# Three edits to the queues of a hybrid layer: 32 constant products, and weight splits and loads that stand behind others

## The chip, the core and the metric

The kernel runs on one core of a Trainium2 chip. A core has five engines with a queue of instructions each: PE (TensorE, matrix products), DVE (VectorE), ACT (ScalarE), POOL (GpSimd) and SP (SyncE), which here only issues DMA transfers. The metric is the device time of one execution in microseconds (us).

## What is computed

One layer of a diffusion backbone on 1024 latent tokens of 1024 channels, with 256 context tokens. Cut to what matters here:

```python
shift, scale, gate = jnp.split(jax.nn.silu(c) @ w_mod[i] + b_mod[i], 3, axis=-1)
mod_c = jax.nn.silu(c_ctx) @ w_mod[i] + b_mod[i]
h = _layer_norm(x) * (1.0 + scale[:, None]) + shift[:, None]
hc = _layer_norm(ctx) * (1.0 + mod_c[D_MODEL:2 * D_MODEL]) + mod_c[:D_MODEL]
u_ctx = hc @ w_in[i][:, :D_SSM] + b_in[i][:D_SSM]
_, ctx_final = _s5_bidir(u_ctx, discs, ssm_c_re[i], ssm_c_im[i], ssm_d[i], None, False)
ua, za, ub, vb, zb, ga, gb = _split_proj(h @ w_in[i] + b_in[i])
y_a, _ = _s5_bidir(ua, discs, ssm_c_re[i], ssm_c_im[i], ssm_d[i], ctx_final, True)
ya = _ssm_glu_gate(y_a, za, glu_w[i], glu_b[i])
yb = _sgu_branch(ub, vb, zb, sgu_ln_g[i], sgu_ln_b[i], sgu_w[i], sgu_b[i], lat_chunks)
out = _merge_out(ya, yb, ga, gb, w_branch_a[i], w_branch_b[i], w_out[i], b_out[i])
x = _layer_norm(DEEPNORM_ALPHA * x + gate[:, None] * out) * ln_g[i] + ln_b[i]
```

`_s5_bidir` is a linear recurrence over the positions, once in each direction (S5). `ua` is its input, `za` its gate.

## The kernel before

Every float32 product is made of three: a value is split into a rounded high half (`hh`, `h_blk`, `uw` 0) and the rest as a low half (`hl`, `l_blk`, `uw` 1), and PE adds high times high, high times low and low times high (L82 to L84). ACT writes the high half of a split and DVE the low half behind it (L77, L78). `modulate` does the same for the rows of the activations: ACT scales and shifts (`hf`), ACT rounds (`hh`), DVE takes the rest (`hl`).

The program begins with loads of x, of the modulation weights `wm` and of the weights for `ua` (`uw`, in four quarters of 256 channels each). While these arrive, PE multiplies constants (`warm`, L455). Then `ua` is computed in steps k = 0 to 7 over 128 channels each, for the first half of the tokens (`ua_step(k, 0)`), and for the second half after it. Ahead of a step's rows stand its modulation: products `pm` on PE, a copy `mrow` on DVE, products `pmc` on PE, an addition `mods` on DVE. A step k uses quarter k/2 of `uw`; `load_uw` loads and splits quarters 1 to 3 in the course of steps 0, 1 and 3. Beside it DVE normalises x tiles 4 to 7 (BATCH_NORM_STATS2 at L185, the normalisation at L197) and prepares the recurrence (`disc`). A later stage does the context.

The recurrence runs on DVE while PE does the products of the other branch. Its readout has four blocks b (`y_mm(b)`): PE multiplies `um` (rows of u, read back from DRAM by `y_rows`) by `mt`, and the states `z` by the tables `ca` (from DRAM by `y_tables`), into `py`. ACT applies GELU from `py` to `gk`, and PE transposes `gk` into `pg` (`y_trans`). `y_states` copies the states to `z` on ACT and DVE. Behind the readout come the products `pp` for `za`, with blocks of weights `r_blk` split to `h_blk` and `l_blk` in the order in which `job` lists them; `weights(key, ahead)` splits all jobs up to `ahead` behind `key`.

The order in which an engine's queue holds its instructions is not that of the text: a scheduler of the tool chain sets it when the program is built. A block under `tc.issue_after(i)` holds instructions that must stand behind instruction i. Loads use rotating buffers (three of RAW, four of TMP, six of WSP), and a load on SP's queue waits until its buffer is free; what stands behind it on SP waits too.

Of the kernel before, what the change touches and what calls it, by code (L numbers as in the profile page):

```python
# [8 lines left out]
F32 = mybir.dt.float32  # L9
F32R = mybir.dt.float32r  # L10
I32 = mybir.dt.int32
AF = mybir.ActivationFunctionType
OP = mybir.AluOpType
# [14 lines left out]
UB, ZB, ZA, GA, GB = 0, 4, 8, 12, 20  # L28
# [8 lines left out]
def mixer_kernel(ctx: ExitStack, tc: tile.TileContext, a, out):  # L37
    nc = tc.nc
    V, S, Pl, PE = nc.vector, nc.scalar, nc.gpsimd, nc.tensor
# [21 lines left out]
    def BANK(name, shape=(128, 512)):  # L61
        return psum.tile(list(shape), F32, name=name, tag="b", bufs=8)

    def dma(o, i):
        return nc.sync.dma_start(o, i)
# [9 lines left out]
    def split(hi, lo, src, eng=None):  # L75

        first = S.activation(hi, src, AF.Copy)  # L77
        return first, (eng or V).tensor_tensor(lo, src, hi.bitcast(F32), op=OP.subtract)  # L78
# [13 lines left out]
    def emit_load():  # L92
        key, ap, shape, eng = jobs[emitted[0]]
        emitted[0] += 1
        raw = RAW("r_" + key, shape)
        dma(raw, ap)
        hi, lo = WSP("h_" + key, shape), WSP("l_" + key, shape)
        split(hi, lo, raw, eng)
        loaded[key] = (hi, lo)

    def weights(key, ahead=2):
        i = [j[0] for j in jobs].index(key)
        while emitted[0] < min(i + 1 + ahead, len(jobs)):
            emit_load()
        return loaded[key]
# [98 lines left out]
    hth = [None] * 8  # L204
    htl = [None] * 8

    def modulate(dh, dl, src, k, n):

        w = src.shape[-1]
        f = TMP("hf")[:, :w]  # L210
        S.activation(f, src, AF.Identity, bias=mods[:, k, 0, n:n + 1], scale=mods[:, k, 1, n:n + 1])
        S.activation(dh, f, AF.Copy)  # L212
        V.tensor_tensor(dl, f, dh.bitcast(F32), op=OP.subtract)

    pms = {}

# [29 lines left out]
    def trans_mod(k, hf):  # L246
        sl = slice(hf * 512, hf * 512 + 512)
        modulate(hth[k][:, sl], htl[k][:, sl], pts[k, hf], k, 0)
# [6 lines left out]
    uw = BIG("uw", (128, BIG0 + 8192), F32R)[:, BIG0:].rearrange("p (s q j n) -> p s q j n", s=2, q=4, j=2)  # L255

    def load_uw(q):
        raw = RAW(f"uw{q}", (128, 2, 512))
        dma(raw, a["w_ua"][q])
        split(uw[:, 0, q], uw[:, 1, q], raw, V)  # L260

    def split_uw0(j):
        return split(uw[:, 0, 0, j], uw[:, 1, 0, j], uwr[:, j], V)
# [87 lines left out]
    q, w, z, sn, cs, odd, eve, sg = (r_[i] for i in range(3, 11))  # L351
# [99 lines left out]


    warm = BANK("warm")
    for i in range(44):
        PE.matmul(warm[:, 0:128], ones, ident, start=True, stop=True)  # L455
    with tc.issue_after(folded.ins):
        for t in range(3):
# [13 lines left out]
    for k in range(8):  # L471
        if k >= 6:
            trans_h(k - 6, 1)
        ua_step(k, 0)
        if k + 2 < 8:
            load_wm(k + 2)

            for t in {2: (4,), 3: (5,), 4: (6, 7)}.get(k, ()):
                load_x(t)
            if k in (0, 1, 3):  # L480
                load_uw((k + 3) // 2)
            trans_pe(k + 2, 0)
            mod(k + 2)
            trans_mod(k + 2, 0)
        for t in {3: (4,), 4: (5,), 5: (6, 7)}.get(k, ()):
            norm_here(t)
        issue(8 if k < 5 else 4)

    xc = []
    for j in range(2):  # L490
        t = RAW(f"xc{j}")
# [5 lines left out]
    def trans_c(k):  # L497
        p = BANK(f"pc{k}")
        for j in range(2):
            PE.transpose(p[:, j * 128:(j + 1) * 128], xc[j][:, k * 128:(k + 1) * 128], ident)  # L500
        modulate(cth[k // 4][:, k % 4, :], ctl[k // 4][:, k % 4, :], p[:, :256], k, 1)
# [26 lines left out]
    for b in range(4):  # L528
        p = BANK(f"pcu{b}")
# [277 lines left out]
            then(t, p, sl)  # L807


    ca_last, cas, mts, ums, zs, gks, gt = {}, {}, {}, {}, {}, {}, []  # L810

    def y_tables(b):
        for d in range(2):
            ca = WSP(f"ca{b}{d}", (128, 8, 8, 16), F32)
            ca_last[b] = dma(ca.rearrange("p g i h -> p (g i h)"), cad[b, d])
            cas[b, d] = ca
        mts[b] = RAW(f"mt{b}", (128, 8, 128))
        if b == 3:

            with tc.issue_after(ca_last[2].ins):  # L820
                dma(mts[b], mtd[b])
        else:
            dma(mts[b], mtd[b])
        if b < 2:
            y_rows(b)

    def y_rows(b):
        src = ud[b].rearrange("t (h g) c -> (t h) g c", g=8)[:, :, 32:160]
        if b < 2:
            t = ROW(f"um{b}", (128, 8, 128))  # L830
            dma(t, src)
            ums[b] = [t[:, g, :] for g in range(8)]
        else:
            ts_ = [TMP(f"um{b}{h}", (128, 4, 128)) for h in range(2)]
            for h, t in enumerate(ts_):
                dma(t, src[:, 4 * h:4 * h + 4])
            ums[b] = [ts_[g // 4][:, g % 4, :] for g in range(8)]

    def y_states(b):
        for d in range(2):  # L840
            zt = G(f"z{b}{d}", (128, 8, 128))
            o = 31 if d == 0 else 33
            for cp in range(2):
                for par in range(2):
                    dst = zt[64 * cp:64 * cp + 64, par:8:2, :]
                    src = vst[64 * par:64 * par + 64, d, o:o + 128, cp, 4 * b:4 * b + 4].rearrange("p c q -> p q c")
                    if par == 0 and cp == 0:
                        S.activation(dst, src, AF.Copy)
                    else:
                        V.tensor_copy(dst, src)  # L850
            zs[b, d] = zt

    def y_mm(b):
        gks[b] = G(f"gk{b}", (128, T, 128))
        for h in range(2):
            p = BANK(f"py{b}{h}", (128, 4, 128))
            for i in range(4):
                g = 4 * h + i
                PE.matmul(p[:, i, :], ums[b][g], mts[b][:, g, :], start=True, stop=False)
                for d in range(2):  # L860
                    PE.matmul(p[:, i, :], zs[b, d][:, g, :], cas[b, d][:, g].rearrange("p i h -> p (i h)"),
                              start=False, stop=d == 1)
            S.activation(gks[b][:, :, 64 * h:64 * h + 64].rearrange("p t (g h) -> p g t h", h=16),
                         p.rearrange("p g (t h) -> p g t h", h=16), AF.Gelu_apprx_tanh)

    def y_trans(b):
        g_ = G(f"gT{b}")
        for h in range(2):
            p = BANK(f"pg{b}{h}")
            for i in range(4):  # L870
                PE.transpose(p[:, 128 * i:128 * i + 128], gks[b][:, 4 * h + i, :], ident)
            dst = g_.rearrange("p (c t) -> p t c", t=T)[:, 4 * h:4 * h + 4, :]
            src = p.rearrange("p (t c) -> p t c", t=4)
            if h == 0:
                S.activation(dst, src, AF.Copy)
            else:
                V.tensor_copy(dst, src)
        gt.append(g_)
# [18 lines left out]
        if i == 6:  # L897
            y_tables(0)

    y_rows(2)  # L900
    y_rows(3)
    for b in range(4):
        y_mm(b)
        if b < 3:
            y_states(b + 1)
        if b < 2:
            y_tables(b + 2)
        if b > 0:
            y_trans(b - 1)
    y_trans(3)  # L910

# [197 lines left out]
    for i in range(0, 8, 2):  # L1111
# [15 lines left out]
        if i == 0:  # L1127

            for h in range(2):
                p = BANK(f"pga{h}")  # L1130
# [141 lines left out]
```

## Time and profile before

| | |
|---|---|
| median of 3 runs | 718.58 us (718.18 to 720.86) |
| profiled execution | 721.4 us, span 719.6 us, mean granted clock 0.991 |
| PE busy | 700.4 us, 97% of the span |
| DVE, ACT, POOL busy | 529.4 us (74%), 248.8 us (35%), 92.6 us (13%) |
| DMA | 101.98 MB, 142 GB/s on average |

The rows that follow come from the profiled execution; its time lies 1.8 us outside the span. Times are in us from the start of the span.

### The profile page before, as it was taken

The page shows a single profiled execution, that of the slowest core. Times are in us where ns is not written, and L with a number is a line of the kernel's source. Part 1 is how long each engine was busy: PE and PEld are TensorE (multiplying, and loading weights), DVE is VectorE, ACT ScalarE, POOL GpSimd, SP SyncE. Part 2 cuts the span into 40 slices and gives each one's busy share as a digit, 9 for nine tenths or more (in the row PEclk, how much of TensorE's full clock was granted, in tenths as well). Part 3 has the DMA queues.
Part 4 walks back from the last instruction along what each step waited for, and adds up shares of the span by engine and source line. Part 5 has one row for each costly group of instructions (what it writes and reads, how often), then busy time and mean ns, then how long its engine had stood idle before and what let it go on. Part 6 is the DMA issues. An engine that isn't in the chain of part 4 may idle for free.

```text
span 719.6 us, 10385 instructions
## 1 busy us (share of the span) xinstructions
PE 700.4 (97%) x3964; PEld 587.3 (82%) x3964; DVE 529.4 (74%) x1148; ACT 248.8 (35%) x360; POOL 92.6 (13%) x145
## 2 busy tenths in 40 slices
PE   9899999999999999999999999999999999999993
PEld 8677898888888888888888898888888878888883
DVE  5489945479889485898988489736678569953993
ACT  4328828741014423111112265414353522310000
POOL 1001142007633000000000000001111000000220
PEclk9999999999999999999999999999999999999997
DMA  7960463625721220121213752234567950251421
GB/s 301 383 231 1 108 170 125 184 89 172 232 64 54 94 88 30 59 89 58 89 60 118 243 205 97 84 125 154 175 203 291 411 205 31 93 172 58 174 90 59
DMA packets 41394, 101.98 MB, mean 142 GB/s; under 512 B 8960, under 2 KB 17792, under 8 KB 41344
## 3 DMA queue, kind: packets, MB, share of 16 engines
q1 hardware_dynamic: 35072, 84.04, 33.9%
q0 software_dynamic: 6272, 17.28, 7.2%
q8 instruction: 31, 0.51, 0.3%
q14 instruction: 19, 0.16, 0.1%
HBM read 79.31 MB, written 24.08 MB: 144 GB/s over the span
## 4 chain that ended last, share of the span: by engine, by line
PE 87%; DVE 5%; DMA 3%; ACT 3%; issue 1%; SPq 0%; POOL 0%; DVEq 0%; ACTq 0%
PE pp L82 10%; PE pp L83 10%; PE pp L84 10%; PE po L1168 4%; PE po L1167 4%; PE po L1166 4%; PE pb L84 4%; PE pb L83 4%; PE pb L82 4%; PE pg L82 4%; PE pg L83 4%; PE pg L84 4%; PE pv L580 3%; DMA uw<-in_w_ua 3%; PE pvb L732 2%; PE pvb L733 2%
## 5 line engine op out<-in xcount | busy, mean ns | idle before, releaser
L82 PE MATMUL pp<-hh,h_blk 128*128 128x512 f32 x320 | 125.3, 392 | 0.0
L83 PE MATMUL pp<-hh,l_blk 128*128 128x512 f32 x320 | 124.6, 389 | 0.0
L84 PE MATMUL pp<-hl,h_blk 128*128 128x512 f32 x320 | 124.5, 389 | 0.0
L82 PEld LDWEIGHTS pp<-hh,h_blk 128*128 128x128 f32 x320 | 60.1, 188 | 13.1 <-ACT vst L582 0.4
L84 PEld LDWEIGHTS pp<-hl,h_blk 128*128 128x128 f32 x320 | 60.1, 188 | 12.6
L83 PEld LDWEIGHTS pp<-hh,l_blk 128*128 128x128 f32 x320 | 60.1, 188 | 12.1
L642 DVE TENSOR_TENSOR scm<-acat,vst 128x128 f32<-128x128 f32 x158 | 46.0, 291 | 9.8 <-ACT vst L582 5.0
L77 ACT ACTIVATE h_blk<-r_blk 128x1024 fp32r<-128x1024 f32 x20 | 21.2, 1061 | 53.7 <-PE pp L83 21.7
L646 DVE TENSOR_TENSOR vst<-vst,scs 128x64 f32<-128x64 f32 x158 | 35.3, 224 | 4.9
L645 DVE TENSOR_TENSOR scs<-scm 128x64 f32<-128x64 f32 x158 | 35.4, 224 | 4.6
L78 DVE TENSOR_TENSOR l_blk<-r_blk,h_blk 128x1024 fp32r<-128x1024 f32 x20 | 24.5, 1225 | 17.7 <-ACT h_blk L77 17.6
L1166 PE MATMUL po<-wobig,mh 128*128 128x512 f32 (+1 forms) x90 | 32.9, 365 | 0.0
L1167 PE MATMUL po<-wobig,mh 128*128 128x512 f32 (+1 forms) x90 | 32.9, 365 | 0.0
L1168 PE MATMUL po<-wobig,ml 128*128 128x512 f32 (+1 forms) x90 | 32.9, 365 | 0.0
L82 PE MATMUL pu<-hh,uw 128*128 128x512 f32 x64 | 27.5, 429 | 3.3 <-ACT hh L212 3.3
L1178 DVE TENSOR_TENSOR r<-po,xr 128x512 f32<-128x512 f32 (+1 forms) x18 | 11.0, 618 | 22.1 <-PE po L1168 22.1
L796 ACT ACTIVATE act<-pp,cols 128x512 f32<-128x512 f32 x16 | 10.9, 678 | 46.5 <-issue 19.0
L69 POOL DMA_DIRECT2D md<-mb x8 | 4.3, 543 | 168.1 <-DVE scs L645 110.7
L84 PE MATMUL pu<-hl,uw 128*128 128x512 f32 x64 | 25.9, 408 | 0.0
L83 PE MATMUL pu<-hh,uw 128*128 128x512 f32 x64 | 25.9, 405 | 0.0
L82 PE MATMUL pb<-yas,h_w_a 128*128 128x512 f32 x64 | 25.3, 395 | 0.0
L733 PE MATMUL pvb<-l_vb,hh 128*128 128x512 f32 x64 | 25.0, 391 | 0.0
(413 smaller groups left out, 1733.1 us busy)
## 6 DMA issues: line engine op xcount, KB each, us to landing
r_blk<-in_w_blk SPq DMA_DIRECT2D x20, 512.0 KB, 3.5
wm<-in_wm SPq DMA_DIRECT2D x16, 512.0 KB, 8.9
x<-in_x SPq DMA_DIRECT2D x8, 512.0 KB, 6.0
cad<-kca POOLq DMA_DIRECT2D x8, 512.0 KB, 3.5
md<-mb POOLq DMA_DIRECT2D x8, 512.0 KB, 3.2
ca<-cad SPq DMA_DIRECT2D x8, 512.0 KB, 5.0
ga<-in_w_blk SPq DMA_DIRECT2D x8, 512.0 KB, 3.5
wgt<-in_w_gate SPq DMA_DIRECT2D x8, 512.0 KB, 3.7
```

Of the source, the lines that this page charges most:

```text
L78: return first, (eng or V).tensor_tensor(lo, src, hi.bitcast(F32), op=OP.subtract)
L82: PE.matmul(o, wh, rh, start=first, stop=False, skip_group_check=more)
L83: PE.matmul(o, wl, rh, start=False, stop=False, skip_group_check=more)
L84: PE.matmul(o, wh, rl, start=False, stop=last, skip_group_check=more)
L580: PE.matmul(p[64 * par:64 * par + 64, c, 0:160], abt[:, 2 * q + par, 64 * c:64 * c + 64], u160[b][:, 2 * q + par, :], start=True, stop=True)
L642: V.tensor_tensor(scm, acat.rearrange("p d (o c) q -> p d o (c q)", o=2), both(n - 1, prev).unsqueeze(2).to_broadcast([128, 2, 2, 32]), op ...
L645: V.tensor_tensor(scs4, m4[:, :, 0, :], m4[:, :, 1, :], op=OP.add)
L646: V.tensor_tensor(both(n, 160 if n == 31 else cur), both(n, cur), scs2, op=OP.add)
L733: PE.matmul(pvb[kk], hth[k][:, ks], wl[:, j, :], start=False, stop=False)
L1166: PE.matmul(p, mh, wh, start=k == 0, stop=False)
L1167: PE.matmul(p, mh, wl, start=False, stop=False)
L1168: PE.matmul(p, ml, wh, start=False, stop=k == 7)
```

## The change

It makes four edits. The series of constant products has 32 instead of 44. The splits of `uw` quarters 1 to 3 must stand behind the last `hh` and the last `hl` that `modulate` has issued so far; their loads don't. The loads of u's rows for blocks 2 and 3 must stand behind the loads of the tables of block 1. In the last pass of the readout's loop `weights` is called for the first block of za's weights (which that point of the program has already split), and the next two blocks are split behind the last `gk` of block 3. (In the changed file all lines behind L207 stand 2 to 9 further down.)

```diff
+    rounded = []
+
     def modulate(dh, dl, src, k, n):
...
-        S.activation(dh, f, AF.Copy)
-        V.tensor_tensor(dl, f, dh.bitcast(F32), op=OP.subtract)
+        rounded.append(S.activation(dh, f, AF.Copy))
+        rounded.append(V.tensor_tensor(dl, f, dh.bitcast(F32), op=OP.subtract))
...
     def load_uw(q):
         raw = RAW(f"uw{q}", (128, 2, 512))
         dma(raw, a["w_ua"][q])
-        split(uw[:, 0, q], uw[:, 1, q], raw, V)
+
+        with tc.issue_after(rounded[-2].ins), tc.issue_after(rounded[-1].ins):
+            split(uw[:, 0, q], uw[:, 1, q], raw, V)
...
     warm = BANK("warm")
-    for i in range(44):
+    for i in range(32):
         PE.matmul(warm[:, 0:128], ones, ident, start=True, stop=True)
...
-            S.activation(gks[b][:, :, 64 * h:64 * h + 64].rearrange("p t (g h) -> p g t h", h=16),
+            gk_last[b] = S.activation(gks[b][:, :, 64 * h:64 * h + 64].rearrange("p t (g h) -> p g t h", h=16),
                          p.rearrange("p g (t h) -> p g t h", h=16), AF.Gelu_apprx_tanh)
...
-    y_rows(2)
-    y_rows(3)
+    with tc.issue_after(ca_last[1].ins):
+        y_rows(2)
+        y_rows(3)
     for b in range(4):
+        if b == 3:
+            weights(f"blk{ZA}", 0)
         y_mm(b)
...
     y_trans(3)
+    with tc.issue_after(gk_last[3].ins):
+        weights(f"blk{ZA}", 2)
```

What stands on ACT's queue in the first steps, before: `uw` with 1024 columns is a split of a quarter, `hf` and `hh` are rows of a step.

```order
8 L211 ACTIVATE hf<-pt_207,mods 128x512
9 L212 ACTIVATE hh_205<-hf 128x512
10 L77 ACTIVATE uw<-uw_272 128x1024
11 L211 ACTIVATE hf<-pt_226,mods 128x512
12 L212 ACTIVATE hh_224<-hf 128x512
13 L77 ACTIVATE uw<-uw_326 128x1024
```

After the change, ACT's queue holds at the same place:

```order
8 L213 ACTIVATE hf<-pt_195,mods 128x512
9 L214 ACTIVATE hh_193<-hf 128x512
10 L213 ACTIVATE hf<-pt_214,mods 128x512
11 L214 ACTIVATE hh_212<-hf 128x512
12 L77 ACTIVATE uw<-uw_260 128x1024
13 L213 ACTIVATE hf<-pt_266,mods 128x512
```

The split of quarter 1 stood between the rows of steps 0 and 1, and now stands behind those of step 1. DVE's queue changed in the same way with the low halves.

On DVE, around the copy `mrow` of step 7 (`lx6s` and `lx7s` are statistics of x tiles 6 and 7, the operation with `lx6m` or `lx7m` on a whole tile is its normalisation), before:

```order
93 L310 TENSOR_TENSOR disc<-disc 128x64
94 L185 BN_STATS lx6s<-x_496 128x6
95 L305 TENSOR_SCALAR disc<-disc 128x64
96 L229 COPY mrow<-pm_565 128x256
97 L185 BN_STATS lx6s<-x_496 128x6
98 L233 TENSOR_TENSOR mods<-pmc_576,cols 128x4
99 L190 BN_AGGR lx6m<-lx6s 128x2
100 L185 BN_STATS lx7s<-x_498 128x6
101 L191 TENSOR_SCALAR lx6m<-lx6m 128x1
102 L185 BN_STATS lx7s<-x_498 128x6
103 L197 TENSOR_SCALAR x_496<-x_496,lx6m 128x1024
```

After the change, DVE's queue holds there:

```order
95 L314 TENSOR_TENSOR disc<-disc 128x64
96 L191 TENSOR_SCALAR lx6m<-lx6m 128x1
97 L185 BN_STATS lx7s<-x_486 128x6
98 L309 TENSOR_SCALAR disc<-disc 128x64
99 L197 TENSOR_SCALAR x_484<-x_484,lx6m 128x1024
100 L314 TENSOR_TENSOR disc<-disc 128x64
101 L190 BN_AGGR lx7m<-lx7s 128x2
102 L309 TENSOR_SCALAR disc<-disc 128x64
103 L191 TENSOR_SCALAR lx7m<-lx7m 128x1
104 L314 TENSOR_TENSOR disc<-disc 128x64
105 L197 TENSOR_SCALAR x_486<-x_486,lx7m 128x1024
106 L231 COPY mrow<-pm_553 128x256
```

The copy (L229, now L231) stood ahead of the second statistics of tile 6; now it stands behind the statistics and the normalisations of both tiles. On PE, twelve transposes for the second half of the tokens that stood within step 7 now stand ahead of it, all together.

At the readout, SP's queue before (blocks of tables `ca`, rows of u `um`):

```order
87 L65 DMA ca_3832<-cad 128x1024
88 L65 DMA ca_3834<-cad 128x1024
89 L65 DMA um_3932<-ud 128x4x128
90 L65 DMA um_3933<-ud 128x4x128
91 L65 DMA um_3936<-ud 128x4x128
92 L65 DMA ca_3895<-cad 128x1024
93 L65 DMA ca_3897<-cad 128x1024
94 L65 DMA um_3937<-ud 128x4x128
```

After the change, SP's queue holds there:

```order
87 L65 DMA ca_3820<-cad 128x1024
88 L65 DMA ca_3822<-cad 128x1024
89 L65 DMA ca_3883<-cad 128x1024
90 L65 DMA ca_3885<-cad 128x1024
91 L65 DMA um_3920<-ud 128x4x128
92 L65 DMA um_3921<-ud 128x4x128
93 L65 DMA um_3924<-ud 128x4x128
94 L65 DMA um_3925<-ud 128x4x128
```

The tables of block 1 (the second pair of `ca`) stood behind three of the four loads of u's rows; now they stand ahead of all four. ACT's queue at the end of the readout, before:

```order
246 L77 ACTIVATE tbig<-fa_4153 128x1024
247 L77 ACTIVATE h_blk_4181<-r_blk_4179 128x1024
248 L863 ACTIVATE gk_4095<-py_4096 128x4x8x16
249 L77 ACTIVATE h_blk_4187<-r_blk_4185 128x1024
250 L863 ACTIVATE gk_4095<-py_4110 128x4x8x16
251 L875 ACTIVATE gT_4124<-pg_4125 128x4x128
252 L875 ACTIVATE gT_4137<-pg_4138 128x4x128
```

After the change, ACT's queue holds there (`gT` and `t13h` are copies and a split for the next stage):

```order
246 L77 ACTIVATE tbig<-fa_4153 128x1024
247 L867 ACTIVATE gk_4083<-py_4084 128x4x8x16
248 L867 ACTIVATE gk_4083<-py_4098 128x4x8x16
249 L879 ACTIVATE gT_4112<-pg_4113 128x4x128
250 L77 ACTIVATE h_blk_4140<-r_blk_4138 128x1024
251 L879 ACTIVATE gT_4125<-pg_4126 128x4x128
252 L77 ACTIVATE t13h_4169<-fa_4165 128x1024
253 L77 ACTIVATE h_blk_4146<-r_blk_4144 128x1024
```

The two `gk` of block 3 stood behind one and two splits of za's weights; now both stand ahead of them.

## Rows read from the trace of the kernel before

**Rows 1.** What PE waited for: us in total, times, the longest.
```profile
PE pu L82 <- ACT hh L212: 3.3, 2, 2.0
...
PE pg L871 <- ACT gk L863: 1.0, 1, 1.0
PE py L861 <- DMA ca<-cad: 0.9, 1, 0.9
```

**Rows 2.** Timeline, DVE and PE at the first modulation (start, duration, engine, line).
```profile
13.89 1.29 DVE L78 TENSOR_TENSOR uw<-uw,uw 128x512 fp32r<-128x512 f32 x2 [0.58 <-ACT uw L77]
...
15.19 0.42 DVE L229 COPY mrow<-pm 128x256 f32<-128x256 f32 x1
...
15.67 0.61 PE L232 MATMUL pmc<-fold,mrow 128*128 128x2 f32 x4
```

**Rows 3.** Timeline at the first and second steps of `ua`.
```profile
22.81 1.06 ACT L77 ACTIVATE uw<-uw 128x1024 fp32r<-128x1024 f32 x1 [4.86 <-DMA uw<-in_w_ua]
...
23.90 1.23 DVE L78 TENSOR_TENSOR uw<-uw,uw 128x1024 fp32r<-128x1024 f32 x1 [4.77 <-ACT uw L77]
...
25.25 0.50 PE L82 MATMUL pu<-hh,uw 128*128 128x512 f32 x1 [2.02 <-ACT hh L212]
...
27.34 0.63 PE L84 MATMUL pu<-hl,uw 128*128 128x512 f32 x1
...
30.32 0.80 PE L244 MATMUL pt<-ident,x 128*128 128x128 f32 x4
```

**Rows 4.** Windows: busy time of each engine, granted clock, DMA share, GB/s.
```profile
core 0: us, PE busy (x) PEld busy (x) DVE busy (x) ACT busy (x) POOL busy (x), PEclk, DMA share, GB/s
10.00:12.00 2.00, 2.00 (x20) 2.00 (x20) 1.45 (x6) 1.69 (x2) 0.92 (x2) 1.00 1.02 420
28.00:30.00 2.00, 2.00 (x6) 1.52 (x6) 1.86 (x4) 0.99 (x2) 0.00 (x0) 0.50 1.02 406
46.00:60.00 14.00, 13.03 (x92) 9.75 (x80) 13.11 (x45) 6.25 (x10) 2.21 (x4) 1.00 0.09 37
460.00:480.00 20.00, 20.00 (x90) 16.57 (x89) 5.37 (x7) 5.44 (x8) 2.16 (x4) 1.00 0.22 80
```

**Rows 5.** Timeline, steps 2, 3 and 7 and the second half's start.
```profile
32.05 0.50 PE L82 MATMUL pu<-hh,uw 128*128 128x512 f32 x1
...
36.91 0.50 PE L82 MATMUL pu<-hh,uw 128*128 128x512 f32 x1
...
51.63 0.42 DVE L229 COPY mrow<-pm 128x256 f32<-128x256 f32 x1
...
53.64 0.68 DVE L185 BATCH_NORM_STATS2 lx7s<-x 128x6 f32<-128x512 f32 x1
...
54.39 0.81 DVE L197 TENSOR_SCALAR x<-x,lx6m 128x1024 f32<-128x1024 f32 x1
...
55.13 0.48 PE L82 MATMUL pu<-hh,uw 128*128 128x512 f32 x1
...
60.32 0.50 PE L82 MATMUL pu<-hh,uw 128*128 128x512 f32 x1 [1.29 <-ACT hh L212]
```

**Rows 6.** Timeline of SP at the start of the readout.
```profile
401.46 3.12 SPq L65 DMA_DIRECT2D um<-ud  x3
...
405.93 0.81 SPq L65 DMA_DIRECT2D ca<-cad  x2
```

**Rows 7.** Timeline of PE, DVE and ACT during the readout.
```profile
412.79 0.46 PE L861 MATMUL py<-ca,z 128*128 128x128 f32 x2 [0.86 <-DMA ca<-cad]
...
417.53 1.23 DVE L923 TENSOR_TENSOR fb<-hh,hl 128x1024 f32<-128x1024 f32 x1 [0.45 <-PE py L859]
...
421.74 4.12 DVE L850 COPY z<-vst 64x512 f32<-64x512 f32 x6
...
430.66 1.08 ACT L77 ACTIVATE h_blk<-r_blk 128x1024 fp32r<-128x1024 f32 x1
...
431.61 0.61 ACT L863 ACTIVATE gk<-py 128x512 f32<-128x512 f32 x1
...
432.27 1.09 PE L871 MATMUL pg<-ident,gk 128*128 128x128 f32 x8 [0.97 <-ACT gk L863]
```

More of the change, by code (lines that the diff above doesn't have):

```diff
@@ L807, in branch @@
             then(t, p, sl)
-    ca_last, cas, mts, ums, zs, gks, gt = {}, {}, {}, {}, {}, {}, []
+    gk_last, ca_last, cas, mts, ums, zs, gks, gt = {}, {}, {}, {}, {}, {}, {}, []
     def y_tables(b):
```

## The prediction

> **What bounds the kernel now.** I began with the list of what TensorE (PE) waited for, because PE is busy for 97% of the span. Three lines of it carry nearly all the idle time that the change could touch [rows 1]: two waits for `hh` (3.3 us together, one of 2.0), one for `gk` (1.0) and one for `ca` (0.9). Then I read the timeline around each. Two places matter: the first 60 us, and the readout of the state space branch at 412 to 433 us. Between and behind them PE works without a gap: in 460 to 480 it is busy 20.00 of 20.00 us, with 90 products, so about 0.22 us for a product of 512 columns at the full clock of 2.4 GHz [rows 4]. A microsecond won at either place therefore reaches the end, unless another engine takes it back within the same stage. DVE is the one to watch there: from 46 to 60 it is busy 13.11 of 14.00 us [rows 4].
>
> **Part 1, 32 constant products in place of 44.** Each is traced as two passes; late in the series 20 passes take 2.00 us, 0.10 us each [rows 4]. Twelve products are 24 passes, so the series ends 24 x 0.10 = 2.4 us sooner. What stands behind it gains nothing from that. The copy `mrow` of step 0 starts on DVE at 15.19 because the split of `uw`, itself held by ACT, occupies DVE from 13.89 for 1.29 us; the product `pmc` on PE starts at 15.67 behind that copy [rows 2]. This chain starts with a load and the change doesn't touch it. So the value is 0. The 2.4 us turn into a hole before 15.67. A gain is excluded by that chain; a loss is not, because of the clock. At 25.25 PE had been idle for 2.02 us, and in 28 to 30 the granted clock was 0.50 (1.2 GHz): seven products took 27.34 to 30.32, which is 2.98 / 7 = 0.43 us each in place of 0.22 [rows 3, 4]. If the new hole does the same, twelve products of `ua_step(0)` cost 12 x (0.43 - 0.22) = 2.5 us. I take 0, since step 1 waited for `hh` anyway and little is lost before 25.25 that isn't covered there; both ends, 0 and 2.5, stay for the range.
>
> The Trainium skill, page TensorE: Matmul & The Clock Gate, section Part 1: The HAM clock gate, says that the slow clock is the default and that activity is what releases it. By that, taking constant products away removes activity for nothing. The row at 0.50 after the hole agrees that the clock is lost by idling; no run here shows yet what this shorter series does. If the page's rule decides at this place, the sum would be worse than mine; a longer stretch of it is the rival called slower.
>
> **Part 2, the weight splits queue behind the rows of the step before.** Before, the ACT queue held the split of `uw` quarter 1 ahead of the rows of step 1. It waited for its load: ACT was idle 4.86 us until 22.81, then split for 1.06, and only then did the rows of step 1 follow, so that PE waited 2.02 us for `hh` until 25.25 [rows 3]. Step 1 doesn't need quarter 1 (step k needs quarter k/2). After, the rows stand ahead of the split. Their inputs are long there, so PE goes straight on at 23.2. The half clock that followed the hole goes too. From step 1 to step 2 PE took 32.05 - 25.25 = 6.80 us, from step 2 to step 3 36.91 - 32.05 = 4.86 [rows 3, 5]; the excess is 1.94. So 2.02 + 1.94 = 3.96 us could come back. One wait replaces part of them: the low half of the split holds DVE from 23.90 for 1.23 us as before [rows 3], the copy `mrow` of step 2 now stands behind it and ends at about 23.90 + 1.23 + 0.42 = 25.55 [rows 2, 3]. PE, which does eight products of step 1 first, is ready for its `pmc` at 23.23 + 8 x 0.22 = 25.0. I take 0.5 for that. The lead at step 2 is 3.96 - 0.5 = **3.5 us**.
>
> Will it last? The scheduler also moved work on DVE. Ahead of the copy `mrow` of step 7 there now stand the second BN_STATS of x tile 6, both of tile 7, and both normalisations, which came behind it: 3 x 0.68 + 2 x 0.81 = 3.66 us [rows 5], with some 0.5 for the small operations between them. DVE has only 14.00 - 13.11 = 0.89 us to spare there [rows 4]. So the copy loses its lead: 51.63 - 3.5 + 3.66 to 4.2 = 51.8 to 52.3, and following DVE's queue instruction by instruction from step 5 gives 52.6. I take 52.6. From that copy to the first product of step 7 the trace has 55.13 - 51.63 = 3.50 us [rows 5]; a first product at 56.1 follows. In the meantime PE does the twelve transposes for the second half, which stood within step 7 and now stand ahead of it. Then the 12 products of step 7 take 12 x 0.22 = 2.7, and the first product of the second half comes at 58.8 without the wait of 1.29 that held it until 60.32 [rows 5]. The gain is **1.5 us**. DVE itself is about 3 ahead there, because the normalisations have been done early, so the next stage isn't held by it and keeps the 1.5. The bounds: 3.5 if DVE's order costs nothing, 0 if the holes at steps 6 and 7 (about 3 us in all by the same reckoning) also cost the clock as the one before 25.25 did. The x loads that now stand ahead of weight loads on SP shift those by one issue each, and step 5 and later need them; I cost that at nothing, with 0.5 us as its price if a load is just in time.
>
> **Part 3, the rows of u behind the tables of block 1.** On SP three `um` loads went out at 401.46 and the tables `ca` of block 1 only at 405.93 [rows 6]. The latter were not late for that reason alone, since they wait for a buffer, but their bytes then queued behind the um bytes, and PE waited 0.86 us for them until 412.79 [rows 7]. After, the tables go at 405.93 with nothing of u ahead of them. The wait goes: 0.86. The um rows leave at about 406.8 to 408.5 and are needed by block 2, six us after the point of that wait; no wait is expected. But the gain doesn't pass whole. The z copies of block 3 hold DVE from 421.74 for 4.12 us, to 425.86 [rows 7], and PE's products of that block need them. DVE had waited only 0.45 us for PE on the way there, at 417.53 [rows 7], so the copies move by 0.45. Between 0.45 and 0.86 I take **0.6**, near the end that DVE sets.
>
> **Part 4, the za weight splits behind the last `gk`.** On ACT the split `h_blk` at 430.66 stands ahead of the last `gk` at 431.61, and another of about the same length ahead of the `gk` before that; PE waited 0.97 us until 432.27 [rows 7]. A split holds the queue for 431.61 - 430.66 = 0.95. After, both `gk` come first, the last one some 1.9 earlier, which more than covers 0.97. The moved splits end on DVE at about 437.8, where their `l_blk` isn't needed until the next block of 48 products is through (48 x 0.22 = 10.6 us from 431.5, so 442). They are covered. DVE has room behind it: 5.37 busy of 20.00 in 460 to 480 [rows 4]. Gain **1.0**; bounds 0.5 and 1.0.
>
> **The sum.** 0 + 1.5 + 0.6 + 1.0 = 3.1 us. The profiled execution took 721.4 us, which makes 718.3; on the median of the three runs, 718.58, it is **715.5**. A difference below 0.5% (3.6 us) can't be told from none here.
>
> **Rivals.**
> *The whole lead is carried.* The order on DVE costs little, because its operations overlap more than their durations add up to. 3.5 + 1.6 = 5.1, so 713.5; with the 0.86 whole, 713.2. For it: PE alone is busy all the time later on. Against it: the 0.89 us to spare on DVE in 46 to 60.
> *The lead is given back.* The holes at steps 6 and 7 cost the clock or one more wait. Only the readout remains: 1.6, so 717.0. For it: two holes of over 1 us each, near the one of 2.02 that did cost the clock. Against it: each is shorter than that one, and a step's products lie between them.
> *Slower.* The shorter series lets the clock fall at the hole before 15.67, and it stays at 1.2 GHz while the projection steps run. Each product costs 0.43 - 0.22 = 0.21 us more. The first 3.5 - 1.5 = 2.0 us of it are covered, since DVE takes that much anyway; the next 3.1 eat the sum. So the kernel is slower from 5.1 / 0.21 = 24 products at half clock on, two whole steps. At three steps (36 products) it would be 7.6 - 5.1 = 2.5 us slower: 721.1. The hole before 25.25 cost seven such products, not 24. The case with 10 to 20 of them ends near 717.
> *The change does nothing at one place* (the tables land as late as before): 0.6 less, within the forecast's own range.
>
> **How the numbers follow.** Forecast 0.45, whole lead 0.25, given back 0.20, slower or no gain 0.10. Faster by over 0.5% means below 715.0: nearly all of the second case and a third of the first, 0.25 + 0.15 = 0.40. Slower by over 0.5% needs more than 722: part of the fourth alone, 0.05. The rest, 0.55, lies within. The range reaches from the second case with some tenths beyond, 712.8, to just the time of before, 718.6; the forecast's own is 714.5 to 716.5.
>
> **What would show it.** In the changed kernel: no wait of 2 us near 23 to 25 and no clock of 0.50 at 28; step 2 near 28.5; waits of PE for `hh` or `mrow` of about a microsecond at steps 6 and 7; the second half starting at 58.8; no wait for `ca` at 412 and none for `gk` at 431. A granted clock of 0.5 anywhere between 16 and 25, or a first product of the second half at 57 or at 60, would show which step was wrong.

## The result and the profile after

The changed kernel takes 723.25 us (median of 14 executions, 721.01 to 724.95), the kernel before in the same rounds 719.26 us (14 executions). The ratio is 1.0053 (95% interval 1.0041 to 1.0066): slower by 0.5%, 4.0 us, where 3 us less were forecast. The profiled execution took 723.99 us with a span of 722.2 us. Of e11 and e12 below one execution each, of 1009.75 and 4017.2 us, is left out of every figure.

The list of PE's waits in the changed kernel (in us: total, times, longest), beside [rows 1]:

```profile
PE pmc L234 <- DVE mrow L231: 2.7, 2, 2.2
PE pu L82 <- ACT hh L214: 2.1, 2, 1.2
PE py L865 <- DMA ca<-cad: 2.0, 2, 1.1
...
PE pm L223 <- DMA wm<-in_wm: 1.5, 2, 0.9
```

Two of the three forecast waits are gone as forecast: the 2.0 us for `hh` before step 1, and `gk`. In their place stands a wait of 2.2 us for `mrow` that was not there before. Where it lies, the timeline of PE shows, and behind it the speed at which PE works on:

```profile
16.30 1.02 PE L234 MATMUL pmc<-fold,mrow 128*128 128x2 f32 x4 [2.17 <-DVE mrow L231]
...
18.20 1.94 PE L223 MATMUL pm<-wm,sc 128*32 128x256 f32 x16
...
21.56 0.77 PE L82 MATMUL pu<-hh,uw 128*128 128x512 f32 x1
```

The windows of the same stretch (columns as in [rows 4]: after the busy times comes PEclk):

```profile
14.00:16.00 2.00, 0.13 (x1) 0.00 (x0) 1.40 (x4) 1.10 (x2) 0.00 (x0) 0.82 0.71 260
16.00:18.00 2.00, 1.70 (x8) 1.57 (x8) 0.41 (x2) 0.45 (x1) 0.00 (x0) 0.50 0.71 267
18.00:20.00 2.00, 2.00 (x18) 0.60 (x16) 0.00 (x0) 0.96 (x2) 0.00 (x0) 0.50 1.03 424
20.00:22.00 2.00, 1.45 (x9) 1.32 (x6) 1.18 (x3) 0.07 (x1) 0.00 (x0) 0.50 1.03 412
22.00:24.00 2.00, 2.00 (x6) 1.52 (x6) 0.60 (x1) 1.97 (x3) 0.00 (x0) 0.50 1.02 416
24.00:26.00 2.00, 2.00 (x8) 1.53 (x6) 1.32 (x2) 0.32 (x1) 0.00 (x0) 0.62 1.02 408
```

The hole lies where the forecast put it, from the end of the first transposes to 16.30. Right behind it the granted clock is 0.50, and it stays there until about 25.5. The 16 products `pm` of step 1, on which its `mrow` and `pmc` wait, take 1.94 us where they take 1.07 at the full clock (in the kernel of e4 below), the four `pmc` 1.02 in place of 0.61 [rows 2]. The first product of step 0 comes at 21.56; its twelve, of which nine run at 0.43 us apiece, end near 26. There is no later stretch below 1.00 near 28, where [rows 4] had one.

Later the changed kernel looks as the prediction drew it, only 4 us late. Step 6 and step 7 wait for `hh` behind DVE's new order:

```profile
52.67 0.50 PE L82 MATMUL pu<-hh,uw 128*128 128x512 f32 x1 [1.24 <-ACT hh L214]
...
60.18 0.50 PE L82 MATMUL pu<-hh,uw 128*128 128x512 f32 x1 [0.89 <-ACT hh L214]
```

And in the readout, the wait for the tables of block 1 [rows 7] is gone, but block 2's tables are late twice, while PE goes through the last transposes `pg` without a stop:

```profile
421.51 0.46 PE L865 MATMUL py<-ca,z 128*128 128x128 f32 x2 [1.14 <-DMA ca<-cad]
422.79 0.46 PE L865 MATMUL py<-ca,z 128*128 128x128 f32 x2 [0.82 <-DMA ca<-cad]
...
434.01 1.94 PE L875 MATMUL pg<-ident,gk 128*128 128x128 f32 x16
```

0.86 + 0.97 us of waits went at the readout and 1.14 + 0.82 came. From the first `py` to the first `pp` it takes 27.3 us in this execution, and 27.2 in that of before.

### The profile page after: what moved, and what is told of

Same layout as the page of the kernel before. It is cut to its first block, busy times and chain, and to the rows that moved or that the text cites. A ratio compares the mean times of both kernels' runs of the same rounds, so it can differ in the third digit from the quotient of the medians.

```text
span 722.2 us, 10336 instructions
## 1 busy us (share of the span) xinstructions
PE 700.5 (97%) x3940; PEld 584.7 (81%) x3940; DVE 527.9 (73%) x1148; ACT 247.8 (34%) x360; POOL 95.0 (13%) x145
## 4 chain that ended last, share of the span: by engine, by line
PE 93%; DVE 2%; DMA 2%; SPq 0%; ACT 0%; issue 0%; POOL 0%; DVEq 0%
PE pp L82 10%; PE pp L83 10%; PE pp L84 10%; PE po L1176 4%; PE po L1175 4%; PE po L1177 4%; PE pb L84 4%; PE pb L83 4%; PE pb L82 4%; PE pg L84 4%; PE pg L82 4%; PE pg L83 4%; PE pv L584 3%; PE pvb L737 2%; PE pvb L736 2%; PE pu L82 2%
```

## The experiments

Theory A: the shorter series leaves a hole on PE before the first `pmc`, there the clock falls to 1.2 GHz, and that costs more than the rest of the change brings. Rival B: the order that the scheduler gave to DVE and PE (statistics and normalisations ahead of `mrow`, holes at steps 6 and 7) costs the time. Rival C: it is the shorter series at the start as such, hole or not. For the readout, theory D: the rows of u hold the tables of block 2 as they held those of block 1. The second column of the table is the number of constant products at the start and in the hole. The last two use the mean granted clock that is recorded for each execution, and set the line at 0.993. That is a rough line: the mean also holds the last us of the run, where the clock is 0.50 behind PE's last product, and it doesn't say where the clock fell. Only a trace does, and each kernel has one.

| kernel | constants | edits of the change that it has | median us (n) | ratio to before, interval | executions below 0.993 | median of the others |
|---|---|---|---|---|---|---|
| before (four rounds pooled) | 44 | none | | 1 | 47 of 122 | 719.25 |
| changed | 32 | all | 723.25 (14) | 1.0053 [1.0041, 1.0066] | 13 of 14 | 721.88 |
| e1 | 44 | uw, rows of u, za | 718.28 (12) | 0.9980 [0.9969, 0.9992] | 1 of 12 | 718.26 |
| e2 | 32 | uw, za | 721.31 (12) | 1.0023 [1.0012, 1.0034] | 12 of 12 | |
| e3 | 44 | uw, za | 717.79 (9) | 0.9977 [0.9962, 0.9992] | 1 of 9 | 717.77 |
| e4 | 32 | none | 722.87 (12) | 1.0038 [1.0024, 1.0052] | 11 of 12 | 719.62 |
| e5 | 32 + 12 | uw, rows of u, za | 719.13 (12) | 0.9978 [0.9966, 0.9990] | 0 of 12 | 719.13 |
| e6 | 32 + 2 long | uw, rows of u, za | 720.14 (12) | 0.9993 [0.9977, 1.0008] | 5 of 12 | 719.07 |
| e7 | 44 + 12 | uw, za | 719.55 (12) | 0.9987 [0.9974, 1.0001] | 0 of 12 | 719.55 |
| e8 | 44 | uw, za, rows of block 3 | 718.14 (12) | 0.9971 [0.9956, 0.9986] | 2 of 12 | 717.70 |
| e9 | 44 + 4 | uw, za | 717.47 (6) | 0.9958 [0.9943, 0.9973] | 0 of 6 | 717.47 |
| e10 | 32 + 8 | uw, za | 721.40 (12) | 1.0002 [0.9980, 1.0023] | 5 of 12 | 717.94 |
| e11 | 44 | uw | 719.47 (11) | 0.9987 [0.9972, 1.0001] | 1 of 11 | 719.38 |
| e12 | 44 | za | 720.12 (11) | 0.9988 [0.9972, 1.0003] | 8 of 11 | 717.69 |
| e13 | 44 + 4 | uw, rows of u, za | 718.10 (11) | 0.9969 [0.9953, 0.9984] | 0 of 11 | 718.10 |
| e14 | 44 + 4 | za | 717.77 (11) | 0.9976 [0.9963, 0.9990] | 0 of 11 | 717.77 |
| e15 (= e9) | 44 + 4 | uw, za | 717.76 (10) | 0.9975 [0.9964, 0.9986] | 0 of 10 | 717.76 |

(The median of e12's others is of three executions, that of the changed kernel's and of e4's of one. The kernels were run in different rounds; each ratio is to the kernel before in the same round.) All experiments compute the whole layer; the constant products feed nothing.

**e1, e2 and e3: parts of the change undone.**

```diff
-    for i in range(32):
+    for i in range(44):        (e1, e3)
...
-    with tc.issue_after(ca_last[1].ins):
-        y_rows(2)
-        y_rows(3)
+    y_rows(2)                  (e2, e3)
+    y_rows(3)
```

> The changed kernel with 44 constant products again. Theory A (the clock): the hole of 2.2 us before the first pmc is gone, the granted clock stays at 1.00 until 23, so the 21 products at 0.43 us of the changed kernel (17 to 25 us) return to 0.22; the second half of the tokens starts near 58.8 in place of 62.9, and the total is about 4 us below the changed kernel, near 719. Rival B (the scheduler's order on DVE and the new holes at steps 6 and 7 cost the time, not the clock): the start of the second half stays within 1 us of 62.9 and the total stays above 722. In both the wait for ca of block 2 near 420 stays.

> The changed kernel with u's rows for blocks 2 and 3 where they were (32 constant products stay). Theory A: the two waits for ca of block 2 (1.14 and 0.82 us) came from the 1 MB of u's rows now between the tables of blocks 1 and 2; they go, the wait of 0.86 for block 1 returns, so the total is about 1.1 below the changed kernel: near 722.1. Rival B: ca of block 2 was late because its buffer came free late; then the waits stay and the total is the changed kernel's plus up to 0.9.

> Both undone: what is left is the order of the uw splits and that of the za splits. Theory A: e1's gain and e2's together, about 5 us below the changed kernel, near 717.5 to 718, so 1.5 to 2.5 below the kernel before (1.0 from the last gk, the rest from the first 60 us). Rival B: about 722 as e2.

44 constants again turn the loss into a gain: 1.0053 to 0.9980, 5.2 us. e2, without the wait for the tables in its profile, still has the loss, and every one of its executions has the low clock. The starts of the readout fit: `py` begins at 403.3 in e1, at 407.1 in e2, at 408.4 in the changed kernel. e3 comes where it was expected. e2 gains more than the 1.1 us expected: its ratio is 0.0030 below that of the changed kernel, 2.2 us, and its trace has no wait for `ca` at all, not even the one of block 1.

**e4: the shorter series alone, in the kernel before.**

```diff
-    for i in range(44):
+    for i in range(32):
         PE.matmul(warm[:, 0:128], ones, ident, start=True, stop=True)
```

> The kernel before with 32 constant products and nothing else. Theory A: the clock falls at the hole before the first pmc; the products of step 0 take 0.43 us, which costs up to 2.5 us, but step 1 still waits for hh behind the weight split, so half of it is covered; 719.5 to 722. Rival B, that the scheduler's order costs the time: the order changes with the series alone, so this one is 722 or more, and the loss arises at steps 6 and 7 and not before 25 us.

It costs 0.38% by itself, and its median of 722.87 is what rival B expected, not theory A's 719.5 to 722. Rival B's first half is true: the number alone gives the scheduler another order, on DVE with the normalisations ahead of step 7's `mrow`, and on ACT with the uw split behind the rows of step 1. In the traces of e4, of e2 and of the changed kernel the queues of all engines hold the same instructions in the same order up to the readout: beside 32 constants the order of the uw splits that the change asks for alters nothing. Theory A's number for e4 had counted on the wait before step 1 as a cover, and that wait is gone here too. But most of the loss is not B's. The profiled execution of e4 happens to be the one of twelve that kept the clock. Here are its windows, and PE behind a hole as long as that of the changed kernel:

```profile
14.00:16.00 2.00, 0.33 (x1) 0.14 (x1) 1.43 (x3) 1.15 (x2) 0.00 (x0) 1.00 0.60 214
16.00:18.00 2.00, 1.52 (x20) 1.18 (x24) 0.59 (x3) 0.68 (x1) 0.00 (x0) 1.00 0.73 274
18.00:20.00 2.00, 1.45 (x18) 0.93 (x11) 1.19 (x3) 0.76 (x3) 0.00 (x0) 1.00 1.04 424
```

```profile
16.48 0.61 PE L232 MATMUL pmc<-fold,mrow 128*128 128x2 f32 x4 [2.15 <-DVE mrow L229]
...
17.51 1.07 PE L221 MATMUL pm<-wm,sc 128*32 128x256 f32 x16
```

The hole before `pmc` is 2.15 us long, the clock 1.00, the `pm` take 1.07 us. The first `py`, in e4 and below it in the changed kernel:

```profile
404.57 0.38 PE L859 MATMUL py<-mt,um 128*128 128x128 f32 x2
```

```profile
408.39 0.38 PE L863 MATMUL py<-mt,um 128*128 128x128 f32 x2
```

The queues up to there are the same, so the lost clock costs 3.8 us in this pair. By the totals of e4 it is 3.3: this execution took 719.62, the median of the other eleven, which lie between 721.23 and 724.14, is 722.89. The order costs about one: the second half of the tokens starts at 59.2 here, and at 57.5 to 58.0 in e1, e3, e11 and e12, which have 44 constants and kept the clock up to there; their `py` begins at 403.1 to 403.7. (That 719.62 is even so near the 719.25 of the kernel before at the full clock is in part the readout: no wait for `ca` fell into it.) And whether a hole of this length costs the clock is not fixed by the program: with the same queues the clock was lost behind holes of 2.17 us (changed kernel) and 2.16 (e2). Of the 38 executions of these three kernels 36 lie below 0.993; of the 44 of e1, e3, e8 and e11, which share another order up to the readout and have 44 constants, five, two of them of e8, whose trace lost it in the readout alone.

**e5, e6, e7: the hole filled.**

```diff
     with tc.issue_after(mod_mm(0).ins):
         trans_pe(0, 0)
+    for i in range(12):        (e5 on the changed kernel, e7 on e3)
+        PE.matmul(warm[:, 0:128], ones, ident, start=True, stop=True)
```

In e6, on the changed kernel, two products of 512 columns stand there:

```diff
+    for i in range(2):
+        PE.matmul(warm, ident, xn[0][:, 0:512], start=True, stop=True)
```

> The changed kernel, with 32 constant products at the start and 12 more placed behind the first transposes, in the hole before the first pmc: the series is as short as in the change, only the hole is filled. Theory A (the clock falls in that hole, in nearly all executions): no product above 0.6 us before 32, the stage of the context's products begins near 84.5 in place of 89.3, and the median falls to that of the kernel with 44 at the start, about 718.3. Rival C (the shorter series at the start itself, by whatever way, costs the time): stays at 721 or more.

> The changed kernel with 32 constant products and two constant float32 products of 512 columns in the hole (about 1.7 us on PE); the copy mrow of step 7 still stands behind the normalisation of x tile 6, unlike with 44. Theory A: no product at half clock before 32; what is left over the kernel with 44 is the price of the order on DVE, 0 to 1.5 us: 718.3 to 720. Rival B (order): 721 or more with the clock at 1.00.

> Only the two orders of weight splits, 44 constant products and 12 more behind the first transposes. Theory A: the last executions that still lose the clock (the one near 721 among nine) go, the spread falls to about 1 us, the median is 717 to 717.8. If the 12 products delay the first pmc instead, it is 718.5 or more, with the first pmc later than 16.0.

The windows of e5:

```profile
14.00:16.00 2.00, 2.00 (x19) 2.00 (x19) 1.41 (x4) 1.15 (x2) 0.00 (x0) 1.00 0.75 272
16.00:18.00 2.00, 2.00 (x24) 1.75 (x27) 0.46 (x2) 0.56 (x1) 0.00 (x0) 1.00 0.66 252
```

With the hole filled PE is busy 2.00 of 2.00 from 14 to 18, no execution of twelve lies below 0.993, and the gain is back though the series at the start is as short as in the change. (Its median of 719.13 is 0.8 above the 718.3 expected; its ratio is that of e1.) Rival C falls. But the order of the scheduler went back with the fill, so e5 alone doesn't exclude B; the one execution of e4 does. e6 has half of B's order (`mrow` of step 7 behind the normalisation of tile 6, ahead of that of tile 7), and in its trace this costs nothing: its second half starts at 56.9 and its `py` at 402.67, no later than in e1. Its median of 720.14 lies just above the 718.3 to 720 expected, but its five executions below 0.993 can't simply be put down to the hole of 0.45 us that it keeps before `pmc`. The profiled one is among them, and its clock stood at 1.00 through the first 60 us; it fell in the readout, behind waits of 1.18 us for `ca` and 0.82 for DVE:

```profile
416.00:418.00 2.00, 1.14 (x8) 1.01 (x9) 1.95 (x4) 0.00 (x0) 0.00 (x0) 1.00 1.01 406
418.00:420.00 2.00, 2.00 (x13) 2.00 (x13) 1.96 (x3) 0.00 (x0) 0.00 (x0) 0.62 0.89 352
420.00:422.00 2.00, 2.00 (x12) 2.00 (x11) 1.94 (x4) 1.08 (x2) 0.00 (x0) 0.53 0.09 35
```

Twelve products are too many: in e5 `pmc` comes at 16.70, in e7 at 17.51 without a wait, and the forecast of 717 to 717.8 for e7 failed, as its second sentence foresaw. The median of e7 is 1.8 above that of e15, which has four; of that 0.1 lies between the rounds, by the kernel before at the full clock.

**e8 and e13: the rows of u.** e8 is e3 with the rows of block 3 alone moved, behind the tables of block 2; e13 is e9 with the rows as the change has them.

```diff
     y_rows(2)
-    y_rows(3)                  (e8)
...
+        if b == 0:
+            with tc.issue_after(ca_last[2].ins):
+                y_rows(3)
```

```diff
-    y_rows(2)                  (e13)
-    y_rows(3)
+    with tc.issue_after(ca_last[1].ins):
+        y_rows(2)
+        y_rows(3)
```

> Only the two orders of weight splits, 44 constant products, and u's rows for block 3 alone moved, behind the tables of block 2. Theory A (the tables wait for the bytes ahead of them): block 1's wait shrinks by half to below 0.8 us, block 2's stays away, so 0.5 to 1 us below the same kernel without the move: 717.0. If the tables' loads are late for another reason (their buffer, the engines' other traffic), the waits stay and the total is 717.8 or more.

> The kernel with 44 + 4 constant products and both orders of splits (e9), and u's rows moved behind the tables of block 1 as in the change; nothing else differs from e9, and the queues of PE, DVE and ACT are the same, instruction by instruction. Theory D (the rows' bytes now lie ahead of the tables of block 2): a wait for ca of block 2 of 1 us or more near 415 to 418, and 0.5 to 1.5 us above the same kernel without the move. The prediction's own term: 0.6 below it. If neither, the move is worth nothing and the waits for ca come and go by execution.

In e13 PE's waits at the readout, and below it those of e15, which differs in SP's queue alone:

```profile
415.52 0.46 PE L867 MATMUL py<-ca,z 128*128 128x128 f32 x2 [0.39 <-DMA ca<-cad]
416.79 0.46 PE L867 MATMUL py<-ca,z 128*128 128x128 f32 x2 [0.82 <-DMA ca<-cad]
```

```profile
409.71 0.46 PE L867 MATMUL py<-ca,z 128*128 128x128 f32 x2 [0.76 <-DMA ca<-cad]
...
422.75 0.46 PE L867 MATMUL py<-ca,z 128*128 128x128 f32 x2 [0.34 <-DMA ca<-cad]
```

1.21 us in the one, at block 2, and 1.10 in the other, at blocks 1 and 3. The medians are 718.10 and 717.76, and the intervals of the ratios overlap almost wholly: the 0.6 that the prediction gave to the move isn't there, and the 0.5 to 1.5 of theory D isn't either. Nor is the place fixed: e5, which has the move, waits 1.15 us at block 1 and not at block 2. The forecast of e8 failed as well: block 1's wait was 2.3 us in its profile, not half, behind it the clock fell to 0.50 at 412 to 414, and its median is no lower than e3's. In all three pairs that differ in these loads alone the kernel with the move is the slower one: by 0.3 us here and 0.5 in e1 against e3 in the medians, and 2.2 by the ratios in the changed kernel against e2. Only in the last pair do the intervals not meet, and there 1.3 us of the traces' difference lie ahead of the readout, where the clock had fallen earlier. So the move gains nothing; whether it costs some tenths is open.

**e9, e10 and e15: a short fill, on e3 (e9, e15) and on e2 (e10).**

```diff
+    for i in range(4):         (8 in e10)
+        PE.matmul(warm[:, 0:128], ones, ident, start=True, stop=True)
     first = split_uw0(0)[0]
```

> Both orders of weight splits, u's rows where they were, 44 constant products and 4 more (about 0.9 us) behind the first transposes. Theory A: the hole before the first pmc is gone, and unlike with 12 more the first pmc isn't delayed (16.3 or sooner, ready copy permitting); all executions at a mean clock of 0.993 or more, and a median 0.3 to 0.8 below the kernel without the 4 (0.9977 of before): 0.9965. If the clock was no longer lost there anyway, no difference.

> The same with 32 at the start and 8 behind the first transposes, so fewer constants in all than before. Theory A: it isn't their number or the early end that counts but the hole: as good as the one with 44 and 4 within 0.5 us, mean clock 0.993 or more in nearly all executions. Rival: 32 at the start lose the clock whatever follows, 721 or more.

> The kernel e9 itself, on the same chip as the two others, which are compared with it: 44 + 4 constant products, both orders of splits, u's rows where they were. 0.996 of the kernel before, all executions at a clock of 0.993 or more.

e9 has the lowest ratio of the study, 0.9958 of before with six executions, and 0.9975 when it was run again as e15. The four products changed the order on DVE as well, so its lead over e3 needn't be the fill's alone. e10 missed: with 32 + 8 five of twelve executions are at 717.4 to 718.0 and seven at 721 to 724, two of these with a mean clock of 0.994 and 0.995. Its profiled execution is one of the five and kept the clock over small holes (0.53 and 0.38 us) at the `pm` and `pmc` of step 0; where the seven lost their time no trace shows.

**e11, e12 and e14: the two orders of splits apart.** e11 has the first of these edits on the kernel before, e12 the second, e14 the second and the four products of e9.

```diff
+        with tc.issue_after(rounded[-2].ins), tc.issue_after(rounded[-1].ins):
+            split(uw[:, 0, q], uw[:, 1, q], raw, V)       (e11)
...
+        if b == 3:
+            weights(f"blk{ZA}", 0)                        (e12, e14)
...
+    with tc.issue_after(gk_last[3].ins):
+        weights(f"blk{ZA}", 2)
```

> The kernel before with the new order of the uw splits alone, 44 constant products. By the prediction's own term 1.5 below before; if the term is right in that the wait of 2.02 and the clock lost behind it go, its executions are nearly all at 0.993 or more, where about half of those of before are at 0.991 or less; the start of the second half comes at 60 to 61, the wait for gk (1.0) stays. If the work moved on DVE takes the gain back: within 0.5 of before.

> The kernel before with the new order of the za splits alone. By the prediction's term 1.0 below before: the wait for gk (0.97) goes and nothing else moves; the same mixture of clocks as before, half of them at 0.991 or less. If the moved splits come late for the products of za, a wait for h_blk or l_blk of up to 1 us appears behind 440 and the total is as before.

> The kernel with 44 + 4 constant products and the order of the za splits, with the uw splits where they were before. Theory E (the order of the uw splits is worth nothing but the clock, which the hole of about 2 us before step 1 loses in about half of the executions): the fast half of its executions is as fast as the kernel with the order, the other half 2 to 3 us slower, at a mean clock of 0.992 or less; the median 1 to 2 above. The prediction's own term: all executions 1.5 above.

e12's profiled execution kept the clock, and from the first `py` to the first `pp` it takes 25.6 us where that of before took 27.2. Of this 1.6 the wait for `ca` of 0.86 us isn't the edit's: it was absent in that execution as it is in those of e4 and e11, which have the za splits where they were and take 26.8 and 26.7. Against these two the za order brings 1.1 us, about its wait for `gk`. e12's three executions at the full clock are 1.6 below those of before; eight of eleven lie below 0.993, more than the half that was expected. e11's executions at the full clock are where those of before are (719.38, 719.25); what it changes is how many lose it, 1 of 11 against 47 of 122. (Its second half starts at 57.5, not at the 60 to 61 expected.) e14 and e15 say the same: without and with the order of the uw splits 717.77 and 717.76. The expectation for e14, that half of its executions would lose the clock in the hole before step 1, failed: none lies below 0.993. That doesn't show that the hole before step 1 is harmless by itself. In e14's trace it is 1.28 us long, in e12's, which has the queues of before, 1.51, and both kept the clock; in that of before it is 2.02, there was no hole before the first `pmc`, and the clock was lost. Why the order has no value of its own, DVE and PE show, e14 first:

```profile
49.68 0.42 DVE L229 COPY mrow<-pm 128x256 f32<-128x256 f32 x1
...
51.77 0.81 DVE L197 TENSOR_SCALAR x<-x,lx6m 128x1024 f32<-128x1024 f32 x1
...
54.18 0.79 DVE L197 TENSOR_SCALAR x<-x,lx7m 128x1024 f32<-128x1024 f32 x1
```

```profile
57.67 0.50 PE L82 MATMUL pu<-hh,uw 128*128 128x512 f32 x1 [0.59 <-ACT hh L212]
```

And e15:

```profile
48.66 0.41 DVE L231 COPY mrow<-pm 128x256 f32<-128x256 f32 x1
...
51.69 0.81 DVE L197 TENSOR_SCALAR x<-x,lx6m 128x1024 f32<-128x1024 f32 x1
...
54.08 0.81 DVE L197 TENSOR_SCALAR x<-x,lx7m 128x1024 f32<-128x1024 f32 x1
```

```profile
57.45 0.50 PE L82 MATMUL pu<-hh,uw 128*128 128x512 f32 x1 [1.40 <-ACT hh L214]
```

With the order, `mrow` of step 7 is a microsecond ahead. But the normalisations of x tiles 6 and 7, which the rows of the second half need, come at the same times in both (51.7 and 54.1), and the second half starts at 57.67 and 57.45. In these two traces DVE's work up to there sets the time, whatever PE gained before.

## Why the prediction was wrong

**Part 1 is the step that failed.** It had the hole before `pmc` right, nearly in length (2.4 us forecast, 2.17 measured), and named the loss of the clock as the other bound. It took 0, because step 1 waited for `hh` anyway. That cover was the very wait that part 2 removes, and that the shorter series removes by itself (e4), so in the changed kernel nothing covered the loss. The sign that the prediction named, a granted clock of 0.5 between 16 and 25, came. The bound was too low as well. It priced the twelve products of step 0 at half clock, 2.5 us. The `pm`, `pmc` and transposes that stand ahead of steps 0 and 1 on the same path slow down too: 0.87 for the `pm` of step 1, 0.4 for each of two groups of `pmc`, about 0.45 for four transposes, and nine products at 0.2, together about 4.0. From e4's kept clock to the changed kernel `py` moves by 3.8. The rival called slower was the right mechanism with the wrong threshold: 24 products of `ua` at half clock were held necessary, because the gain of part 2 was to be eaten first; nine were enough, with what else ran at 1.2 GHz. Its chance of 0.10 had been read from one trace, in which a hole of 2 us cost seven products.

**Part 2**, 1.5 us: the wait and the half clock near 28 went, but the value is 0 at the full clock (e14 against e15, and e11 against before). What the trace of before showed as 1.94 us of a step's excess was one execution's lost clock, which 75 of 122 executions, by their mean clock, don't have; I took it as a property of the program, and subtracted the gain from a median of three of which two, 718.18 and 718.58, are as fast as the executions at the full clock. With 44 constants the lead is lost in the wait for `hh` at the second half (1.40 us in e15, 0.59 in e14); with 32 DVE's order takes more than the lead: the second half starts at 59.2 in e4 against 58.0 in e12. The bound named there, that the holes at steps 6 and 7 cost the clock, didn't come true: in the changed kernel it is 1.00 from 26 us on until PE's last products.

**Part 3**, 0.6 us: no gain measured. The step that fails is "no wait is expected" for block 2. **Part 4**, 1.0: right, 1.1 us by the readout's length in e12 against e4 and e11.

**The order on DVE** was put down to the uw splits. The scheduler made it of the shorter series (e4 has it, e3 hasn't), and its price is about a microsecond, by the one trace of e4. Added up as an estimate, 719.25 for before at the full clock, 3.8 for the lost clock, 1 for the order and 1.1 less for the za splits make 723.0, against 723.25 measured. The 0.5% below which the prediction saw no difference was too coarse: the intervals above are 0.1 to 0.2% to either side.

The Trainium skill's rule that was weighed in part 1 (page TensorE: Matmul & The Clock Gate, section Part 1: The HAM clock gate), that the slow clock is the default and activity releases it, stood on the side of what came. The traces agree: the granted clock is 0.50 behind the hole of the changed kernel, and 1.00 in e5, where products fill that place. In e4 it stayed at 1.00 over the unfilled hole, so the rule gave the direction and not the outcome of a single execution.

## What to carry to other kernels

Count holes on PE near the start before taking filler work away: a hole that delays nothing can cost the clock, and then PE's part of every chain behind it takes up to twice as long (here 1.94 us in place of 1.07). After a change in the number of filler products compare the order of all queues: the scheduler may have made another one. A cover counts only if no other part of the same change removes it. Where executions of one program differ by some us, look at the mean clock of each before reading a single profile: a stretch at half clock in one trace may be absent in most executions, and a gain read from it belongs to the chance of losing the clock and not to the edit.

## What was not expected of the hardware

With the same queues up to the readout the clock was kept over a hole of 2.15 us in one trace (e4, 719.62) and lost behind 2.17 and 2.16 us in two (the changed kernel, 723.99, and e2, 721.08); the eleven other executions of e4, which have no trace, took 721.2 to 724.1. In the kernel before 47 of 122 executions lie below a mean clock of 0.993, at 721.04 in the median against 719.25; of the two traces with its queues up to the readout the one (before) lost the clock behind a hole of 2.02 us and the other (e12) kept it over one of 1.51. With the hole before step 1 removed (e11) or the place before the first `pmc` filled (e14) hardly any do: 1 of 11 and 0 of 11. The readout can lose it as well (e6, e8). What in an execution decides is open. The clock isn't all either: e10, e11 and e14 have executions 2 to 4 us above the median of their others at a mean clock of 0.993 to 0.995, and no trace caught one.
